# One core of Trainium2: the second product of the attention's scores on 128 rows instead of 64

## The chip, the cores and the metric

The kernel runs on one core of one Trainium2 chip. The metric is the device time of one execution in microseconds (us), as the median of several runs. TensorE (PE) multiplies, its weight loads (PEld) are recorded apart, VectorE (DVE) and ScalarE (ACT) work on elements, GpSimd (POOL) is a third engine for elements, and the queue of SyncE (SP) issues the DMAs.

## The reference

One decoder layer with 1024 tokens and 1024 channels. What the change touches is the differential attention with 4 heads: each head has two maps of scores (queries and keys of 64 channels each, two sets of them), and the two softmaxes are subtracted.

```python
def diff_attention(q1, q2, k1, k2, v, rel_bias, lam):
    ...
        s1 = jnp.einsum('bhqd,bhkd->bhqk', qb1, k1f) * scale + bias
        s2 = jnp.einsum('bhqd,bhkd->bhqk', qb2, k2f) * scale + bias
        p1 = jax.nn.softmax(jnp.where(mask, s1, -1e30), axis=-1)
        p2 = jax.nn.softmax(jnp.where(mask, s2, -1e30), axis=-1)
        return jnp.einsum('bhqk,bhkd->bqhd', p1 - lam * p2, vf)
```

Around it stand a projection `rmsnorm(x) @ w_in`, a pooling and a short convolution beside the attention, the output product `w_o`, a SwiGLU block and a last norm. All data are float32.

## The kernel before

Products are made in three passes: every operand is split into a high half and a low half of few enough bits (float32r), and high x high, high x low and low x high are summed in PSUM. `split_exact` and its relatives do this: ScalarE copies the high half, VectorE subtracts it from the source.

The scores save one pass by stacking halves on the partitions. A query tile `q_tiles[hd, c]` (512 queries) holds for the map s the high half on 64 of the 128 partitions (`ROWS[s]`) and the low half on the other 64. A key tile `k_tiles[hd, c]` holds the high half on both. So one matmul of 128 rows (L496) sums high x high and low x high. The keys' low halves of both maps stand in one tile per head, `k_low[hd]`, map s on the partitions `ROWS[s]`, and a second matmul of 64 rows (L497) adds high x low into the same PSUM bank.

`scores(hd, i)` works on a block of 128 queries and the keys up to it: for each map and each 512 keys, the pair L496, L497; then VectorE adds the bias and takes the maximum (L501, L504, L507), ScalarE takes the exponential (L509), VectorE weighs the two maps (L512, L514, L515). `flip` transposes the result on TensorE (L527) and splits it on ScalarE (L529) and VectorE (L530). `attend` multiplies by v (L540), normalises with an inverse root from GpSimd (`rstd`, L110), and `put` scales on VectorE (L550) and transposes (L552).

The order is written by hand. One iteration of the loop over `early` puts an older block, scores block n, flips and attends block n - 1, and between these it issues steps of a list of projections (`fill_to`, `pace`), which are matmuls of 128 rows (L248, L261, and L199 for v). For each head this list has a column of keys (`done_k`), then a column of queries (`done_q`). The last head's remaining blocks run beside the output product (L616). Then come gate and up (L907) and down (L1016).

Large tiles live in 35 slots of 4 KB per partition (`Slots`), handed out in the order in which they were given back: `sl.new` takes the oldest free slot, `sl.done` returns one. A tile in a reused slot waits for the last readers of the tile before it.

Of the kernel before, what the change touches and what calls it, by code (L numbers as in the profile page):

```python
# [35 lines left out]
# One operand pair per matmul pass: (stationary half, moving half).  # L36
# [11 lines left out]
def split_exact(nc, hi, lo, src, lo_eng):  # L48
    """src = hi + lo exactly, each with few enough bits for a one-pass product."""
    nc.scalar.copy(hi, src)  # L50
    lo_eng.tensor_sub(lo, src, hi.bitcast(F32))  # L51


class Slots:
    """4 KB-per-partition pieces of SBUF, handed out in the order in which they were given back."""
# [16 lines left out]
def tile_hybrid_block(ctx, tc, x, g_mix, w_in, lq1, lk1, lq2, lk2, subln_g, rel_bias, w_pool,  # L72
# [17 lines left out]
    # The tensor engine's clock rises while the first tokens are on their way.  # L90
# [33 lines left out]
    def h_tiles(place):  # L124
        """(hi, lo) for each half of the tokens: [channel in block, block, token]."""
        return [tuple(grp.tile([P, KT, 512], F32R, tag=f"g{2 * place[c] + a}", name=f"h{c}{a}") for a in range(2))
                for c in range(2)]
# [11 lines left out]
    def turn_split(hn, h, t, ks, ps):  # L139
        """h[:, ks, t] = transpose(hn), split; the two instructions that end it."""  # L140
        hi, lo = h[t // 4]
        cols = slice((t % 4) * P, (t % 4 + 1) * P)
        for n, k in enumerate(range(KT)[ks]):
            nc.tensor.transpose(ps[:, n, :], hn[:, k * P:(k + 1) * P], ident)
        return (nc.scalar.copy(hi[:, ks, cols], ps),
                nc.vector.tensor_sub(lo[:, ks, cols], ps, hi[:, ks, cols].bitcast(F32)))

    def transposed(hn, h, t, whole=True):
        """h[:, :, t] = transpose(hn), split; hn is given back."""
        if whole:  # L150
            r = turn_split(hn, h, t, slice(0, KT), bank("a", (P, KT, P)))
        else:
            for n in range(2):
                r = turn_split(hn, h, t, slice(4 * n, 4 * n + 4), bank("c", (P, 4, P)))
        sl.done(hn)
        return r
# [6 lines left out]
    def halves_of(raw, shape, pin=False):  # L163
        """A loaded block of weights as two exact halves."""
        hi = sl.new("w_hi", shape, F32R)
        lo = sl.new("w_lo", shape, F32R)
        ins = nc.scalar.copy(hi, raw)
        if pin:
            tc.keep_in_program_order(ins)
        nc.vector.tensor_sub(lo, raw, hi.bitcast(F32))  # L170
        sl.done(raw)
        return hi, lo
# [69 lines left out]
    def project(w, done):  # L242
        """128 columns of h @ w_in, transposed; done(c, ps) takes each half of the tokens."""
        for c in range(2):
            ps = bank("f")
            for k in range(KT):
                for j, (a, b) in enumerate(PASSES):
                    nc.tensor.matmul(ps, w[a][:, k, :], h[c][b][:, k, :], start=k == 0 and j == 0,  # L248
                                     stop=k == KT - 1 and j == 2)
                yield  # L250
            done(c, ps)
        sl.done(*w)

    def project_pair(ws, dones, between):
        """Two blocks of columns, both for the first half of the tokens before the other half."""
        for c in range(2):
            for w, done in zip(ws, dones):
                ps = bank("f")
                for k in range(KT):
                    for j, (a, b) in enumerate(PASSES):  # L260
                        nc.tensor.matmul(ps, w[a][:, k, :], h[c][b][:, k, :], start=k == 0 and j == 0,  # L261
                                         stop=k == KT - 1 and j == 2)
                    yield
                done(c, ps)
            if c == 0:
                between()
        for w in ws:
            sl.done(*w)
# [7 lines left out]
    def qk_columns(hd):  # L276
        # Both maps' halves side by side on the partitions: [hi; lo] of the first, [lo; hi] of the second.
# [7 lines left out]
        # The high halves of each map twice on the partitions, the low halves of both once.  # L285
        def done_k(c, ps):
            if c == 0:
                k_low[hd] = sl.new("k_low", (P, 2, 512), F32R)
            low = k_low[hd]
            t = k_tiles[hd, c] = sl.new("k", (P, 2, 512), F32R)  # L290
            for s, (own, other) in enumerate((ROWS, ROWS[::-1])):
                nc.scalar.copy(t[own, s, :], ps[own])
                nc.vector.tensor_sub(low[own, c, :], ps[own], t[own, s, :].bitcast(F32))
                nc.vector.tensor_copy(t[other, s, :], t[own, s, :])

# [95 lines left out]
    def chain(items):  # L391
        """Steps of projections, the next one's weights ahead of each one's products.

        What a projection leaves to do (the pool's windows) is spread over the ones after it."""
# [90 lines left out]
    def scores(hd, i):  # L485
# [4 lines left out]
        for s in range(2):  # L490
            ps = bank("a", (P, S))
            q = q_tiles[hd, i // 4][:, s, (i % 4) * P:(i % 4 + 1) * P]
            for c in range((n + 511) // 512):
                w = min(512, n - c * 512)
                part = ps[:, c * 512:c * 512 + w]
                nc.tensor.matmul(part, q, k_tiles[hd, c][:, s, :w], start=True, stop=False)  # L496
                nc.tensor.matmul(part, q[ROWS[s]], k_low[hd][ROWS[s], c, :w], start=False, stop=True)  # L497
# [82 lines left out]
    def split_mixed(c, ms):  # L580
        """Both halves of some of the mixed channels, for one half of the tokens."""
# [44 lines left out]
    # Gate and up are products of 2 by 2 blocks (weights' columns and the channels; the channels and the tokens) in  # L626
    # Winograd's form of Strassen's seven block products. B11, B21: channels of both halves, tokens 512 to 1023;
    # B12, B22: tokens 0 to 511.
# [4 lines left out]
    def split_to(tiles, ps, cols):  # L633
        """Two blocks of 128 channels into each of the tiles."""
        for n, (hi, lo) in enumerate(zip(*tiles)):
            split_exact(nc, hi[:, :, cols], lo[:, :, cols], ps[:, 2 * n:2 * n + 2], nc.vector)

    def turn_early(t):
        """Columns of B11 and B21."""
# [18 lines left out]
    def attend_block():  # L658
        if flipped:
# [3 lines left out]
            for c in over.get((hd, i), ()):  # L663
                sl.done(q_tiles[hd, c], k_tiles[hd, c], v_tiles[hd, c])
                if c == 0:
                    sl.done(k_low[hd])
# [71 lines left out]
    def fetch(m):  # L738
        """Two neighbouring blocks of 128 columns, as two halves of the channels."""
# [44 lines left out]
    def add_rows(t):  # L784
        """The sums of blocks for 128 tokens: T1 = B12 - B11, T2 = T3 + B11, T3 = B22 - B12, T4 = B21 - T2."""
# [74 lines left out]
    # The operands of the last product, two pairs of blocks together: [pair, operand, row, column].  # L860
    kept = {}

    def store(j, names, src):
        """Operands on their way to DRAM: [row, operand, column]."""
# [4 lines left out]
    def store_hidden(j, top, low):  # L869
        """Blocks of the hidden values (tokens; channels) and the sums of them."""  # L870
# [12 lines left out]
    def down_sums(j):  # L883
        """The sums of the blocks (channels; columns) of w_down."""
# [12 lines left out]
    def unit(m, name):  # L897
        """One of the seven products, and what it lets the other engines do."""
# [95 lines left out]
    # Block 1 of the tokens is 512 to 1023; the pairs of blocks of channels are summed two pairs at a time.  # L994
# [24 lines left out]
    def add(i, two, half, ps):  # L1019
        """x2 += ps for a block of tokens and half of the channels."""  # L1020
# [4 lines left out]
    def close(t, r, scaled=False):  # L1025
        """out = x2 * r * g_final; the first half of x2 may have been multiplied by g_final before."""
# [11 lines left out]
    # What of x2 each product is added to, by (second block of tokens, second half of the channels).  # L1038
# [17 lines left out]
    for name in NAMES:  # L1056
# [9 lines left out]
        if final:  # L1066
            # The last block of tokens in two pieces, so that what follows the last product is short.
# [65 lines left out]
def _constants():  # L1133
    """Tables that depend on shapes alone: distances' buckets, the causal mask, window lengths."""
# [33 lines left out]
```

## Time and profile before

| | |
|---|---|
| median of 3 runs | 1117.84 us (1117.19 to 1118.68) |
| span of the profiled execution | 1115.0 us; no other time is given for it |
| TensorE busy | 98% of the span |
| weight loads | 80% |
| VectorE busy | 67% |
| ScalarE busy | 39% |
| GpSimd busy | 4% |

The span runs from the first to the last instruction. A busy share is the union of the times of an engine's instructions; matmuls overlap each other, so the distance between the starts of two of them says more than their lengths. Times in rows are counted from the span's start.

### The profile page before, as it was taken

The page shows a single profiled execution, that of the slowest core. Times are in us where ns is not written, and L with a number is a line of the kernel's source. Part 1 is how long each engine was busy: PE and PEld are TensorE (multiplying, and loading weights), DVE is VectorE, ACT ScalarE, POOL GpSimd, SP SyncE. Part 2 cuts the span into 40 slices and gives each one's busy share as a digit, 9 for nine tenths or more (in the row PEclk, how much of TensorE's full clock was granted, in tenths as well). Part 3 has the DMA queues.
Part 4 walks back from the last instruction along what each step waited for, and adds up shares of the span by engine and source line. Part 5 has one row for each costly group of instructions (what it writes and reads, how often), then busy time and mean ns, then how long its engine had stood idle before and what let it go on. Part 6 is the DMA issues. An engine that isn't in the chain of part 4 may idle for free.

```text
span 1115.0 us, 13835 instructions
## 1 busy us (share of the span) xinstructions
PE 1097.5 (98%) x5215; PEld 896.9 (80%) x5215; DVE 745.7 (67%) x1321; ACT 429.3 (39%) x764; POOL 47.8 (4%) x73
## 2 busy tenths in 40 slices
PE   7999999999999999989999999999999999999997
PEld 7887777797777777868888888888888888888886
DVE  6549567657677565698786768677776668565554
ACT  6325435444544333552332333132323335344342
POOL 1000000000000001120000000000000000000011
PEclk9999999999999999999999999999999999999999
DMA  7301111001125232213554354435544897466553
GB/s 254 102 24 56 39 38 58 19 1 49 39 80 194 76 133 76 91 51 113 198 188 162 111 190 172 162 119 171 179 148 135 294 347 252 155 219 196 190 182 139
DMA packets 96131, 150.60 MB, mean 135 GB/s; under 512 B 7321, under 2 KB 48833, under 8 KB 96065
## 3 DMA queue, kind: packets, MB, share of 16 engines
q1 hardware_dynamic: 96064, 149.72, 40.1%
q8 instruction: 41, 0.67, 0.2%
q14 instruction: 26, 0.20, 0.1%
HBM read 107.49 MB, written 43.00 MB: 135 GB/s over the span
## 4 chain that ended last, share of the span: by engine, by line
PE 94%; DVE 3%; issue 1%; ACT 1%; DMA 0%; POOL 0%; POOLq 0%; DVEq 0%; ACTq 0%
PE ps_f L907 16%; PE ps_f L248 14%; PE ps_a L907 11%; PE ps_c L907 9%; PE ps_a L1016 9%; PE ps_f L616 6%; PE ps_c L1016 5%; PE ps_f L1016 5%; PE ps_f L199 4%; PE ps_a L497 3%; PE ps_c L540 3%; PE ps_a L496 3%; PE ps_f L261 2%; PE ps_c L527 1%; PE ps_a L616 1%
## 5 line engine op out<-in xcount | busy, mean ns | idle before, releaser
L51 DVE TENSOR_TENSOR lo<-raw,hi 128x1024 fp32r<-128x1024 f32 (+1 forms) x84 | 93.0, 1132 | 78.3 <-ACT hi L50 75.9
L248 PE MATMUL ps_f<-h,w_hi 128*128 128x512 f32 x448 | 143.0, 400 | 0.4 <-ACT pt L385 0.4
L50 ACT CAST hi<-raw 128x1024 fp32r<-128x1024 f32 (+1 forms) x84 | 81.5, 980 | 118.2 <-DMA raw<-in_w_down 30.3
L907 PE MATMUL ps_c<-b,w 128*128 128x512 f32 x528 | 124.4, 390 | 0.0
L907 PEld LDWEIGHTS ps_c<-b,w 128*128 128x128 f32 x528 | 98.8, 188 | 20.3
L248 PEld LDWEIGHTS ps_f<-h,w_hi 128*128 128x128 f32 x448 | 80.7, 188 | 19.4 <-issue 2.7
L248 PE MATMUL ps_f<-h,w_lo 128*128 128x512 f32 x224 | 87.5, 391 | 0.0
L110 POOL TENSOR_TENSOR rstd<-ms,nhalf 128x1 f32<-128x1 f32 x56 | 34.6, 618 | 1049.4 <-DVE ms L103 958.5
L51 DVE TENSOR_TENSOR w<-raw,w 128x512 fp32r<-128x512 f32 x66 | 46.5, 705 | 47.5 <-ACT w L50 47.3
L616 PE MATMUL ps_f<-wo_hi,mix 128*128 128x512 f32 x224 | 76.2, 404 | 0.2 <-DVE raw L623 0.2
L50 ACT CAST w_hi<-s 128x1024 fp32r<-128x1024 f32 x44 | 46.0, 1053 | 62.4 <-DVE s L772 55.1
L50 ACT CAST w<-raw 128x512 fp32r<-128x512 f32 x66 | 41.0, 622 | 60.0 <-PE ps_f L907 27.3
L907 PE MATMUL ps_f<-T,w 128*128 128x512 f32 x264 | 63.7, 390 | 0.0
L509 ACT ACTIVATE e<-ps_a,nm 128x128 f32<-128x128 f32 (+7 forms) x64 | 47.2, 744 | 36.8 <-DVE nm L507 36.8
L51 DVE TENSOR_TENSOR w_lo<-s,w_hi 128x1024 fp32r<-128x1024 f32 x44 | 53.4, 1218 | 11.1 <-DMA kept8S<-sum 2.6
L907 PEld LDWEIGHTS ps_f<-T,w 128*128 128x128 f32 x264 | 49.4, 188 | 10.8 <-DVE low L920 0.6
L1016 PE MATMUL ps_a<-lo,hi 128*128 128x512 f32 (+1 forms) x154 | 57.6, 374 | 0.0
L1016 PE MATMUL ps_a<-hi,lo 128*128 128x512 f32 (+1 forms) x154 | 57.6, 374 | 0.0
L1016 PE MATMUL ps_a<-hi 128*128 128x512 f32 (+1 forms) x154 | 57.5, 374 | 0.0
L907 PE MATMUL ps_f<-t,w_hi 128*128 128x512 f32 x176 | 54.5, 389 | 0.0
L907 PE MATMUL ps_a<-t,w_hi 128*128 128x512 f32 x176 | 54.2, 389 | 0.0
L907 PE MATMUL ps_f<-b,w_hi 128*128 128x512 f32 x176 | 54.2, 389 | 0.0
(203 smaller groups left out, 2325.9 us busy)
## 6 DMA issues: line engine op xcount, KB each, us to landing
raw<-in_w_down SPq DMA_DIRECT2D x37, 512.0 KB, 4.5
raw<-in_w_gate SPq DMA_DIRECT2D x22, 512.0 KB, 6.0
raw<-in_w_up SPq DMA_DIRECT2D x22, 512.0 KB, 3.8
raw<-in_w_in SPq DMA_DIRECT2D x20, 512.0 KB, 3.7
raw<-in_x SPq DMA_DIRECT2D x16, 512.0 KB, 4.1
raw<-in_w_o SPq DMA_DIRECT2D x8, 512.0 KB, 5.2
x<-raw SPq DMA_DIRECT2D x8, 512.0 KB, 2.6
x<-x SPq DMA_DIRECT2D x8, 512.0 KB, 5.9
```

Source lines behind the costliest of these rows:

```text
L50: nc.scalar.copy(hi, src)
L51: lo_eng.tensor_sub(lo, src, hi.bitcast(F32))
L110: nc.gpsimd.tensor_tensor(r, ms, nhalf, op=ALU.pow)
L199: nc.tensor.matmul(ps[:, tt, :], h[t // 4][b][:, k, cols], ws[k // 4][a][:, k % 4, :], start=k == 0 and j == 0, stop=k == KT - 1 and j == 2)
L248: nc.tensor.matmul(ps, w[a][:, k, :], h[c][b][:, k, :], start=k == 0 and j == 0, stop=k == KT - 1 and j == 2)
L496: nc.tensor.matmul(part, q, k_tiles[hd, c][:, s, :w], start=True, stop=False)
L497: nc.tensor.matmul(part, q[ROWS[s]], k_low[hd][ROWS[s], c, :w], start=False, stop=True)
L509: nc.scalar.activation(es[:, :n], ps[:, :n], AF.Exp, bias=nm, scale=1.0, accum_out=z[:, s:s + 1])
L540: nc.tensor.matmul(av[:, :(2 - a) * DV], pts[j // 4][:, a, (j % 4) * P:(j % 4 + 1) * P], rhs, start=j == 0 and a == 0, stop=j == i and a == 1)
L616: nc.tensor.matmul(wo_ps[t][nh], halves[m, t // 4][:, a, cols], wo[m][b][:, nh * 512:(nh + 1) * 512], start=m == SET_A[0] and j == 0, stop ...
L907: nc.tensor.matmul(ps, w[a][:, k, :], h[b][k], start=new and k == 0 and j == 0, stop=k == 3 and j == 2, skip_group_check=not new)
L1016: nc.tensor.matmul(ps, a_op[a][:, j, i * P:(i + 1) * P], b_op[b][:, j, cols], start=start and p == 0, stop=stop and p == 2, skip_group_che ...
```

## The change

The low halves of the keys get a tile for each half of the tokens, `k_low[hd, c]`, with the two maps side by side in the free dimension and each map on both halves of the partitions. VectorE writes one half of the partitions as before, GpSimd copies it to the other. The second product then takes the whole query tile as its stationary operand and 128 rows of low halves; it adds low x low to the sum. One more slot is taken per head, and the low halves are given back with the queries, keys and values of their half of the tokens. The rest of the diff removes comments.

```diff
         def done_k(c, ps):
-            if c == 0:
-                k_low[hd] = sl.new("k_low", (P, 2, 512), F32R)
-            low = k_low[hd]
             t = k_tiles[hd, c] = sl.new("k", (P, 2, 512), F32R)
+            low = k_low[hd, c] = sl.new("k_low", (P, 2, 512), F32R)
             for s, (own, other) in enumerate((ROWS, ROWS[::-1])):
                 nc.scalar.copy(t[own, s, :], ps[own])
-                nc.vector.tensor_sub(low[own, c, :], ps[own], t[own, s, :].bitcast(F32))
+                nc.vector.tensor_sub(low[own, s, :], ps[own], t[own, s, :].bitcast(F32))
                 nc.vector.tensor_copy(t[other, s, :], t[own, s, :])
+                nc.gpsimd.tensor_copy(low[other, s, :], low[own, s, :])
...
                 nc.tensor.matmul(part, q, k_tiles[hd, c][:, s, :w], start=True, stop=False)
-                nc.tensor.matmul(part, q[ROWS[s]], k_low[hd][ROWS[s], c, :w], start=False, stop=True)
+                nc.tensor.matmul(part, q, k_low[hd, c][:, s, :w], start=False, stop=True)
...
             for c in over.get((hd, i), ()):
-                sl.done(q_tiles[hd, c], k_tiles[hd, c], v_tiles[hd, c])
-                if c == 0:
-                    sl.done(k_low[hd])
+                sl.done(q_tiles[hd, c], k_tiles[hd, c], k_low[hd, c], v_tiles[hd, c])
```

## Rows read from the trace of the kernel before

**Rows 1.** Page: the span.
```profile
span 1115.0 us, 13835 instructions
```

**Rows 2.** Page: the chain that ended last, by engine.
```profile
PE 94%; DVE 3%; issue 1%; ACT 1%; DMA 0%; POOL 0%; POOLq 0%; DVEq 0%; ACTq 0%
```

**Rows 3.** Stretches: length, PE, PEld, DVE, ACT, POOL busy, granted clock, DMA share, GB/s.
```profile
84.00:112.00 28.00, 28.00 (x125) 21.26 (x125) 25.18 (x68) 15.53 (x40) 1.66 (x3) 1.00 0.20 57
...
76.00:436.00 360.00, 359.49 (x1766) 281.85 (x1766) 242.03 (x621) 159.09 (x386) 22.10 (x37) 1.00 0.19 63
```

**Rows 4.** Timeline of TensorE, block (2,7): start, length, engine, line, operation, shapes.
```profile
306.57 0.50 PE L496 MATMUL ps_a<-k,q 128*128 128x512 f32 x1
307.00 0.49 PE L497 MATMUL ps_a<-k_low,q 64*128 64x512 f32 x1
...
309.12 0.73 PE L248 MATMUL ps_f<-h,w_hi 128*128 128x512 f32 x2
309.69 0.39 PE L248 MATMUL ps_f<-h,w_lo 128*128 128x512 f32 x1
```

**Rows 5.** Timeline of the weight loads there; in brackets the idle time before.
```profile
307.00 0.18 PEld L497 LDWEIGHTS ps_a<-k_low,q 64*128 64x128 f32 x1 [0.24 <-issue]
...
309.46 0.19 PEld L248 LDWEIGHTS ps_f<-h,w_lo 128*128 128x128 f32 x1
```

**Rows 6.** Timeline of TensorE in gate and up, 15 matmuls apart.
```profile
599.92 0.39 PE L907 MATMUL ps_a<-t,w_lo 128*128 128x512 f32 x1
...
603.32 0.39 PE L907 MATMUL ps_f<-b,w_lo 128*128 128x512 f32 x1
```

**Rows 7.** Timeline of TensorE: scores of 384, 256 and 128 columns.
```profile
131.30 0.44 PE L496 MATMUL ps_a<-k,q 128*128 128x384 f32 x1
131.67 0.44 PE L497 MATMUL ps_a<-k_low,q 64*128 64x384 f32 x1
...
245.29 0.38 PE L497 MATMUL ps_a<-k_low,q 64*128 64x256 f32 x1
...
245.92 0.38 PE L497 MATMUL ps_a<-k_low,q 64*128 64x256 f32 x1
...
108.75 0.32 PE L497 MATMUL ps_a<-k_low,q 64*128 64x128 f32 x1
109.00 0.50 PE L496 MATMUL ps_a<-k,q 128*128 128x512 f32 x1
```

**Rows 8.** Timeline of TensorE: products of 128 rows with 256 and 128 columns.
```profile
249.55 0.28 PE L199 MATMUL ps_f<-w_lo,h 128*128 128x256 f32 x1
...
250.63 0.28 PE L199 MATMUL ps_f<-w_lo,h 128*128 128x256 f32 x1
...
309.92 0.93 PE L527 MATMUL ps_c<-ident,e 128*128 128x128 f32 x7
```

**Rows 9.** Timeline of VectorE and GpSimd, before gate and up.
```profile
476.97 0.69 DVE L791 TENSOR_TENSOR t<-hn 128x512 f32<-128x512 f32 x1
...
478.87 1.63 POOL L792 TENSOR_TENSOR t<-hn,t 128x512 f32<-128x512 f32 x1
479.26 1.78 DVE L789 TENSOR_TENSOR t<-hn 128x512 f32<-128x512 f32 x1
```

**Rows 10.** Timeline, block (0,2): first score, weighing, transpose.
```profile
90.94 0.39 PE L496 MATMUL ps_a<-k,q 128*128 128x384 f32 x1
...
97.80 0.62 DVE L515 SCALAR_TENSOR_TENSOR e<-e,t 128x384 f32<-128x384 f32 x1
...
101.82 0.49 PE L527 MATMUL ps_c<-ident,e 128*128 128x128 f32 x3
```

**Rows 11.** Timeline where head 1 ends and head 2 begins.
```profile
240.29 1.08 ACT L529 CAST pT<-ps_c 128x512 fp32r<-128x512 f32 x2
...
242.26 0.34 DVE L515 SCALAR_TENSOR_TENSOR e<-e,t 128x128 f32<-128x128 f32 x1
...
243.14 1.63 PE L540 MATMUL ps_c<-v,pT 128*128 128x256 f32 x13
```

## The prediction

> **What bounds the kernel now.** I read the page first. The chain of work that ended last lies on TensorE for 94% [rows 2] of a span of 1115.0 us [rows 1], so time taken off TensorE's queue counts, as long as no other engine becomes the later one. The second reading is the table by stretches: the scores run from about 76 to 436 us, and there TensorE is busy for 359.49 of 360 us while VectorE is busy for 242.03 [rows 3]. A busy TensorE is not a TensorE at its peak, however, so the third reading is the timeline, for the distance from one matmul's start to the next.
>
> In a block of full length the first products (128 rows) and second products (64 rows) alternate, all 512 columns wide, and start 0.425 us apart (six distances from 306.57 to 309.12 us [rows 4]). The record of the weight loads shows why: the load of each second product begins together with its matmul, at 307.00, after 0.24 us in which the loader waited for nothing the profile shows. Where only 128-row products follow each other, the load for 309.69 begins at 309.46, under the matmul ahead of it [rows 5]. In gate and up, 15 matmuls of 128 rows and 512 columns start between 599.92 and 603.32 us, 0.227 us apart, weight loads and all [rows 6]. The granted clock is 1.00 (2.4 GHz) over the whole stretch of the scores [rows 3], so the clock doesn't explain the difference. What distinguishes the slow pairs is that 128 and 64 rows alternate, and the first matmul after a second product pays too: L248 at 309.12 and its successor take 0.57 us where two take 0.45.
>
> **The change, part by part.** *The second product gets 128 rows.* The number of matmuls and their columns stay; every L497 now has the shape of L496, and no matmul of the attention changes the number of rows. By the loops of scores() L497 runs 96 times: for 4 heads and 2 maps, six products of 512 columns and two each of 384, 256 and 128 over the eight blocks, which makes 48, 16, 16 and 16; L496 does the same. Per width, the distance now and the distance between 128-row matmuls:
> 512 columns: 0.425 against 0.227 us, 0.198 saved, x96 = 19.0 us.
> 384: 0.37 [rows 7]; no 128-row reference, so I take the middle of 0.12 and 0.227, 0.173; 0.197 x32 = 6.3 us.
> 256: 0.315 [rows 7] against 0.12 (L199, nine matmuls from 249.55 to 250.63 [rows 8]); 0.19 x32 = 6.1 us.
> 128: 0.25 [rows 7] against 0.11 (seven transposes of L527 take 0.93 us, three take 0.49 [rows 8, 10]: four more add 0.44); 0.14 x32 = 4.5 us.
> Together 35.9 us. At the ends of a block's scores the distances differ a little: leaving them costs the following matmul 0.11 us today, and the first product of a block meets no switch. For 32 blocks that is +3.5 and about as much in the other direction, so I keep 36 us, with 33 and 39 as bounds.
> Two pages of the Trainium skill differ here. "TensorEngine Tiling (Array Packing)", section Key Properties, says that changing the tiling mode drains the engine; by it the saving is that of the rows. "TensorE: Matmul & The Clock Gate", section "Why this matters for your kernels", says that a single matmul with K=32 takes as long as one with K=128; by that rule alone 64 rows would cost nothing extra and the change would give 0 us. The trace, with 0.425 against 0.227 us, agrees with the first for alternating rows.
>
> *Sixteen copies on GpSimd* (two per call of done_k; 64x512, one input). The trace has none of this kind. From below they cost nothing, since a key column is finished a whole query column ahead of its first scores. From above: GpSimd's L792, 128x512 with two inputs, takes 1.63 us, and a VectorE instruction with two SBUF inputs under it stretches from 0.69 to 1.78 us [rows 9]. Sixteen copies that each hold VectorE up for 1.6 us make 26 us of VectorE time; 242 + 26 = 268 of some 324 us is still not a bound on average. "SBUF — State Buffer", section "Who interferes with whom", calls this an exclusive lock that the later one waits for in full, which agrees with 1.78.
> It can hurt only where VectorE is late already. That is 84 to 112 us (25.18 of 28 us busy [rows 3]), where head 1's keys are split, with four copies. The weighted block of head 0's third block of queries ends on VectorE at 98.42 and TensorE's transpose of it starts at 101.82 [rows 10]: 3.4 us of cover. Four held-up instructions are up to 6.4 us, and the faster TensorE eats about 1 us of the cover per block. GpSimd also gives rstd (L110), and VectorE's L550 queues behind it, with flips and the key splits behind that. I take 1.5 us of loss, bounds 0 and 4 here and 26 for all heads.
>
> *One tile more per head.* Counting new() and done() through the program's order, the free slots of 35 are fewest where block (2,0) follows block (1,7): three are free when the last pT of (1,7) is taken. With heads 1 and 2 both live there are two fewer, so that pT gets the slot of an e of (2,0), which is free only when L515 at 242.26 has ended (242.60). The first attend of (1,7) is at 243.14 [rows 11], and its second pT is read some 0.5 us later, so a copy and a subtract after 242.60 (half of the 1.08 us that L529's pair takes, and about the 0.69 us of [rows 9]) fit nearly. Cost 0 to 1.5 us; I take 0.5. Releasing the low halves with the other tiles of their half merely reorders slots.
>
> *The rest:* the DMAs are the same, the PSUM banks too. Gate, up and down lie behind the attention and move forward as a whole. I take 0.5 us for small waits that come to light in 324 us.
>
> **Sum.** 36 - 1.5 - 0.5 - 0.5 = 33.5 us. The span is 1115.0 us and the median of the runs is 1117.84, so 2.8 us lie around the span; the page gives no other time for the profiled execution, and I keep the 2.8. 1115.0 - 33.5 + 2.8 = 1084.3 us.
>
> **Rivals.**
> A (0.75): as worked out, with 36 +- 3 on TensorE and 0 to 6 us given back: 33 - 6 = 27 to 39, so 1079 to 1091 us. For it: no other engine is above 242 of 360 us.
> B (0.16): VectorE's lateness eats part of it. Each copy holds VectorE for up to 1.6 us, and of these 26 us more than the 6 of A reach TensorE: 36 - 6 to 36 - 26 saved, so more than about 1088 (I draw the line at 1091) and up to 1108 us. For it: 84 to 112 us is nearly full, and in-order VectorE passes a wait on. Against it: outside that stretch VectorE has a third of its time free.
> C (0.04): the change doesn't do what it says: the distance belongs to two products into one bank by one stationary operand, not to the rows. Then 1118 us, or up to 2 more with the copies. Against it: L248 writes 24 products into one bank without it, and the matmul after the pair, in another bank, is hit as well.
> D (0.05): the slots run out, on the other side. With two fewer, the e's of blocks (1,4) to (2,0) could land on slots whose reader belongs to the block before, so that each block's scores wait for the softmax ahead of them. From the first score of block (0,2) at 90.94 to the end of its L515 at 98.42 [rows 10] that is 7.5 us; five blocks lose 37.5 us: 1084.3 + 37.5 = 1121.8 us. It decides only from nearly all five in full, since 33.5 us stand on the other side; the four longer blocks would take more than 7.5 us each. Against it: by the count one slot is still free, and it is one pT that lands on a younger tile, not the e's.
>
> **How the numbers follow.** About 0.2% (2 us) is what a measurement of this kernel can tell from no change. A and B are faster by more: 0.91. C is within: 0.04. D is slower: 0.05. The likeliest case gives 1084.3; its own range is 1079 to 1091. The range for 8 in 10 takes A and half of B: 1079.5 to 1100.
>
> **What would show it.** Right: L497 reads 128x512, its distance to the next matmul falls to 0.227 us, its weight loads start under the matmul before, the "issue" idle time at L496 and L497 is gone, and the last scores come some 33 us earlier. The copies show on GpSimd, with some VectorE instructions near them stretched. Wrong: distances that stay at 0.425 (C); new idle time of TensorE before L527, L540 or L552 released by VectorE (B); or before L496 or L540 at the change from head 1 to head 2 (D).

## The result, and the profile after

The changed kernel takes 1085.03 us (median of 4 runs, 1083.01 to 1085.60) against 1118.26 us before: a ratio of 0.9707, 95% interval 0.9691 to 0.9723, or 33.2 us less. A second measurement (experiment 8) gave 0.9696 (0.9678 to 0.9714). The span of the profiled execution fell from 1115.0 [rows 1] to 1083.3 us.

First the timeline of TensorE over a block of full length, to be laid beside [rows 4] (start, length; the second product is now L496, the first L495):

```profile
283.40 0.39 PE L495 MATMUL ps_a<-k,q 128*128 128x512 f32 x1
283.63 0.39 PE L496 MATMUL ps_a<-k_low,q 128*128 128x512 f32 x1
283.85 0.39 PE L495 MATMUL ps_a<-k,q 128*128 128x512 f32 x1
...
284.76 0.62 PE L248 MATMUL ps_f<-h,w_hi 128*128 128x512 f32 x2
285.21 0.39 PE L248 MATMUL ps_f<-h,w_lo 128*128 128x512 f32 x1
```

Six products of the scores and two of the projection take 285.21 - 283.40 = 1.81 us. In [rows 4] the same eight take 309.69 - 306.57 = 3.12 us. The weight loads there:

```profile
283.18 0.19 PEld L495 LDWEIGHTS ps_a<-k,q 128*128 128x128 f32 x1
283.40 0.19 PEld L496 LDWEIGHTS ps_a<-k_low,q 128*128 128x128 f32 x1
```

The load for the product that starts at 283.63 begins at 283.40, under the product ahead of it. In [rows 5] the load of a second product began with its own product, after 0.24 us of "issue"; that idle time is gone.

The products of 384 columns, for which there was no reference ahead, start 0.17 and 0.18 us apart. The rows are from a block of 896 keys, whose first 512 columns follow in the second map:

```profile
272.82 0.34 PE L495 MATMUL ps_a<-k,q 128*128 128x384 f32 x1
272.99 0.34 PE L496 MATMUL ps_a<-k_low,q 128*128 128x384 f32 x1
273.17 0.40 PE L495 MATMUL ps_a<-k,q 128*128 128x512 f32 x1
```

Not all that TensorE saved came out. The list of waits of the weight loads from 76 to 410 us (who waited for whom: us in total, times, longest) has new entries:

```profile
PEld ps_c L526 <- ACT ps_c L118: 1.8, 2, 1.0
PEld ps_c L526 <- ACT att L562: 1.8, 2, 1.2
PEld ps_f L615 <- ACT mix L50: 1.1, 1, 1.1
PEld ps_f L248 <- DVE w_lo L170: 0.9, 1, 0.9
```

L526 are the transposes of a scored block. They wait for a PSUM bank that `attend` and `put` of older blocks still use on ScalarE: L118 squares the result of `attend` into its bank, L562 reads the bank of `put`. The table by stretches, up to the last attend of each kernel, shows the same from the other side (columns as in [rows 3]; first the kernel before, then the one after):

```profile
76.00:443.40 367.40, 366.67 (x1798) 287.50 (x1798) 246.88 (x631) 161.68 (x393) 23.91 (x39) 1.00 0.20 64
```

```profile
76.00:410.10 334.10, 329.96 (x1799) 281.99 (x1798) 243.71 (x630) 161.12 (x393) 30.70 (x49) 1.00 0.22 70
```

VectorE has nearly the same work in less time, and TensorE is no longer busy all the time: it is idle for 334.10 - 329.96 = 4.1 us where it was idle for 0.7, so 3.4 us of what its products saved did not come out.

What came out can be read off the last attend, again before and after (minimum, median and longest length in ns, first and last start):

```profile
L540 PE MATMUL ps_c<-v,pT x288: 221/280/385, 90.8 to 443.4; 128*128 128x256 f32 x80, 128*128 128x128 f32 x64
```

```profile
L539 PE MATMUL ps_c<-v,pT x288: 221/278/384, 90.2 to 410.1; 128*128 128x256 f32 x80, 128*128 128x128 f32 x64
```

The attention ends 443.4 - 410.1 = 33.3 us earlier. What lies behind it took 1115.0 - 443.4 = 671.6 us and takes 1083.3 - 410.1 = 673.2 us, 1.6 us more. Of the 33.3 us some 1.7 are not the change: in the profiled execution of the kernel before, TensorE's clock fell once during the attention, in that of the changed kernel it did not (last section). Experiment 1, whose products are those of the kernel before and whose profile has no such fall either, starts its last attend at 441.8, 31.7 us behind the changed kernel.

The copies are there as well, on GpSimd (mean 786 ns), and the mean of VectorE's casts beside them has grown from 422 to 468 ns; the third line is that cast in the kernel before:

```profile
L293 POOL CAST k_low<-k_low 64x512 fp32r<-64x512 f32 x16 | 12.6, 786 | 73.5 <-DVE k_low L291 73.5
...
L292 DVE CAST k<-k 64x512 fp32r<-64x512 f32 x16 | 7.5, 468 | 0.5
```

```profile
L294 DVE CAST k<-k 64x512 fp32r<-64x512 f32 x16 | 6.8, 422 | 0.5
```

The mean hides that only two of the sixteen casts grew, to 0.85 and 0.73 us. In these two the copy had started first (85.30 against 85.34 us, and 86.98 against 87.14) and took 0.61 us. Where the cast started first, by 0.03 or 0.10 us, it kept its 0.42 us and the copy beside it took 0.79 to 0.87.

### The profile page after: what moved, and what is told of

Read it like the earlier page. It is cut to its first block, busy times and chain, and to the rows that moved or that the text cites. A ratio compares the mean times of both kernels' runs of the same rounds, so it can differ in the third digit from the quotient of the medians.

```text
span 1083.3 us, 13855 instructions
## 1 busy us (share of the span) xinstructions
PE 1061.3 (98%) x5215; PEld 891.2 (82%) x5215; DVE 745.1 (69%) x1321; ACT 428.1 (40%) x764; POOL 61.4 (6%) x89
## 4 chain that ended last, share of the span: by engine, by line
PE 84%; DVE 9%; DMA 3%; ACT 2%; issue 1%; POOL 0%; POOLq 0%; SPq 0%; DVEq 0%; ACTq 0%
PE ps_f L904 17%; PE ps_a L904 11%; PE ps_f L248 10%; PE ps_c L904 10%; PE ps_a L1013 9%; PE ps_f L615 6%; PE ps_c L1013 5%; PE ps_f L1013 5%; PE ps_f L199 4%; PE ps_c L539 2%; PE ps_c L526 1%; PE ps_a L496 1%; PE ps_a L495 1%; PE ps_f L261 1%; DVE k_low L291 1%
## 5 line engine op out<-in xcount | busy, mean ns | idle before, releaser
L248 PE MATMUL ps_f<-h,w_hi 128*128 128x512 f32 x448 | 140.8, 395 | 0.6 <-ACT pt L384 0.6
```

## The experiments

The times of each group were taken beside runs of the kernel before on the same chip, and the ratio is to those.

**1. The layout without the products.** The changed kernel, with only the second product put back to 64 rows:

```diff
-                nc.tensor.matmul(part, q, k_low[hd, c][:, s, :w], start=False, stop=True)
+                nc.tensor.matmul(part, q[ROWS[s]], k_low[hd, c][ROWS[s], s, :w], start=False, stop=True)
```

> All of the change except its products: the low halves stand twice, with the copies on GpSimd and the extra tile per head, but the second product reads only its 64 rows. Theory (the gain is the 192 changes between 128 and 64 rows, about 0.2 us each, and the copies and tiles cost a little): 1118.3 us plus 0 to 3, so 1118 to 1121, with the distance of full-width products still near 0.425 us. Rival (the gain comes from the new layout, the slots or the order of releases): near 1085 us.

Measured: 1118.06 us, ratio 1.0002 (0.9990 to 1.0014). The copies, tiles and releases cost 0.2 us, give or take 1.3, and win nothing, in a kernel whose second products still have 64 rows. In the timeline the distance is back:

```profile
306.42 0.50 PE L495 MATMUL ps_a<-k,q 128*128 128x512 f32 x1
306.85 0.49 PE L496 MATMUL ps_a<-k_low,q 64*128 64x512 f32 x1
307.27 0.50 PE L495 MATMUL ps_a<-k,q 128*128 128x512 f32 x1
```

The whole gain is in the number of rows of the second product.

**2. The products without the layout.** The kernel before, with a second product of 128 rows that multiplies the high halves of the keys again; it leaves their low halves out of the scores:

```diff
-                nc.tensor.matmul(part, q[ROWS[s]], k_low[hd][ROWS[s], c, :w], start=False, stop=True)
+                nc.tensor.matmul(part, q, k_tiles[hd, c][:, s, :w], start=False, stop=True)
```

> The products alone: the kernel before, whose second product has 128 rows and multiplies the high halves of the keys a second time, so that the low halves are left out of the scores; no copies and no extra tiles. Theory (36 us gross, 2 to 4 us of them given back by copies, tiles and late VectorE): 1082 us, 2 to 4 under the changed kernel. Rival (the copies and tiles are free and the missing part of the gross gain is lost to other waits): the same as the changed kernel, 1085 us within 1.

Measured: 1086.59 us, ratio 0.9725 (0.9710 to 0.9739). Without copies and extra tiles it is not faster than the changed kernel. The theory that they take 2 to 4 us falls, and the rival's number, 1085 us within 1, is missed by 0.6; the missing part of the gross gain goes to other waits. They are not the same ones: here the largest was 2.7 us of the weight loads before L616, for a copy on ScalarE, which the changed kernel has with 1.1 us, and the clock fell behind it (last section). Up to the last attend TensorE is idle for 4.35 us, about as long as in the changed kernel (4.1).

**3. Half as many changes of rows in long blocks.** The kernel before, 64 rows, with the loop over pieces of 512 keys split in two:

```diff
-            for c in range((n + 511) // 512):
-                w = min(512, n - c * 512)
-                part = ps[:, c * 512:c * 512 + w]
+            parts = [(c, ps[:, c * 512:min(n, c * 512 + 512)], min(512, n - c * 512)) for c in range((n + 511) // 512)]
+            for c, part, w in parts:
                 nc.tensor.matmul(part, q, k_tiles[hd, c][:, s, :w], start=True, stop=False)
+            for c, part, w in parts:
                 nc.tensor.matmul(part, q[ROWS[s]], k_low[hd][ROWS[s], c, :w], start=False, stop=True)
```

> The kernel before with 64 rows, but in blocks of more than 512 keys both first products of a map come ahead of both second ones. That leaves out 64 of the 192 changes of rows (4 heads, 4 blocks, 2 maps, 2 changes). Theory (each change costs about 0.2 us): 64 x 0.2 = 12.8 us less, 1105.5 us, and two neighbouring second products of 64 rows start about 0.227 us apart. Rival (64 rows as such are slow): still about 1118 us, and neighbouring 64-row products 0.42 us apart. Rival (two products in a row into one bank): all 36 us or more of these blocks' share gone, with first and second products 0.227 us apart everywhere in them.

Measured: 1106.03 us, ratio 0.9913 (0.9879 to 0.9947). By the ratio that is 9.7 us less (5.9 to 13.5), by the medians 11.4; one of the four runs took 1112.13 us, the others 1105.03 to 1106.74. 12.8 lies inside the interval, 0 and 36 do not. The timeline of one block shows what a change consists of:

```profile
309.30 0.73 PE L497 MATMUL ps_a<-k_low,q 64*128 64x512 f32 x2
309.96 0.73 PE L495 MATMUL ps_a<-k,q 128*128 128x512 f32 x2
310.63 0.73 PE L497 MATMUL ps_a<-k_low,q 64*128 64x512 f32 x2
311.29 0.73 PE L261 MATMUL ps_f<-h,w_hi 128*128 128x512 f32 x2
311.86 0.39 PE L261 MATMUL ps_f<-h,w_lo 128*128 128x512 f32 x1
```

Every pair takes 0.66 to 0.67 us until the next pair, whether it has 64 or 128 rows; two products without a change take 0.454. So a change costs 0.21 us and 64 rows as such cost nothing. The last line splits it: the pair of L261 is left without a change and takes 0.57, so 0.11 us stand at the entry, where the first load begins together with its own product, and the other 0.09 to 0.10 at the end of the pair before. My expectation of 0.227 us between two neighbouring 64-row products missed: they start 0.34 us apart (310.63 and 310.97), and so do the two of 128 rows ahead of them (309.96 and 310.30), since the first of each pair carries its own exposed load. That the engine empties at a change is the likely reason for the other part; the rows show only its length.

**4. The copies on ScalarE.**

```diff
-                nc.gpsimd.tensor_copy(low[other, s, :], low[own, s, :])
+                nc.scalar.copy(low[other, s, :], low[own, s, :])
```

> The changed kernel with the sixteen copies on ScalarE in place of GpSimd. Theory (copies on GpSimd hold VectorE up by a lock and delay rstd, which costs 1 to 3 us): 1082 to 1084 us, and VectorE's cast beside them back at 0.42 us. Rival (the loss is elsewhere): 1085 us or up to 2 more, since ScalarE gets 16 copies of about 0.58 us more in the stretch where it is also needed.

Measured: 1086.54 us, ratio 0.9726 (0.9711 to 0.9740). No gain, although all sixteen casts of VectorE are back at 0.42 us: that VectorE and GpSimd hinder each other in the copies costs no time that shows here. ScalarE has the copies instead (0.62 us each), so a gain below what that costs could be hidden; the theory's 1 to 3 us in the total did not come.

**5. Second products of both maps side by side.** The kernel before, 64 rows; all first products of a block, then the second ones in turn on partitions 0 to 63 and 64 to 127:

```diff
...
                 nc.tensor.matmul(part, q, k_tiles[hd, c][:, s, :w], start=True, stop=False)
-                nc.tensor.matmul(part, q[ROWS[s]], k_low[hd][ROWS[s], c, :w], start=False, stop=True)
+                order.append((c, s, q, part, w))
+        for c, s, q, part, w in sorted(order, key=lambda o: o[:2]):
+            nc.tensor.matmul(part, q[ROWS[s]], k_low[hd][ROWS[s], c, :w], start=False, stop=True)
...
```

> The kernel before with 64 rows; per block all first products of both maps come ahead, then the second products, alternating between map 0 (partitions 0 to 63) and map 1 (64 to 127). Two changes of rows per block in place of four or eight: 64 changes in all against 192. Theory (a change costs 0.1 us for the array to empty and 0.11 us for a weight load that cannot run ahead, and 64 rows as such cost nothing): 128 x 0.2 = 25.6 us under the kernel before, 1092 us, second products 0.227 us apart. Rival 1 (products on different halves of the rows run side by side): pairs of second products start nearly together, 48 x 0.2 to 0.227 us or some 8 us more saved, 1084 us, level with the changed kernel. Rival 2 (64-row products pay the weight load each): second products 0.335 us apart, some 5 us less saved than the theory, 1097 us. In each case up to 2 us come on top because VectorE gets the first map later.

Measured: 1088.82 us, ratio 0.9738 (0.9719 to 0.9757). The timeline decides for the first rival in the products themselves:

```profile
285.03 0.73 PE L499 MATMUL ps_a<-k_low,q 64*128 64x512 f32 x4
285.69 0.73 PE L248 MATMUL ps_f<-h,w_hi 128*128 128x512 f32 x2
286.26 0.40 PE L248 MATMUL ps_f<-h,w_lo 128*128 128x512 f32 x1
```

Four second products take 0.66 us, as long as two did in experiment 3, and they start two by two, at 285.03 and at 285.37: products on different halves of the rows run at the same time. The Trainium skill says so too ("TensorE: Matmul & The Clock Gate", Part 3), and the 0.66 us agree. The rival's 1084 us did not come, however: the kernel is some 4 us behind the changed one. In blocks of up to 512 keys it saves one product of 0.11 to 0.227 us and pays two changes, 0.4 us: 16 blocks lose about 0.2 us each, 3 us, worked out from the rows and not tried apart. The trace agrees in size: the distances from all 192 score products and from the matmul behind each block to their next ones sum to 47.0 us, in the changed kernel to 44.8 without its waits. A wait of 2.33 us and a stretch at half clock behind it (last section) stand in this execution too.

**6. Transposes later.** The changed kernel with `PACE = (0.3, 1.0)` in place of `(0.15, 1.0)`:

> The changed kernel, with 30% in place of 15% of each block's projections issued ahead of the transposes of the block before. Theory (the 4 us that TensorE now waits in the attention are late results of VectorE and ScalarE, which flips and attends meet 1 us earlier per block than before): the transposes get about 1 us more cover and the attends 1 us less, 1 to 2 us saved, 1083 to 1084 us. Rival (the waits are for banks and tiles of other stages, or move from flip to attend): within 1 us of the changed kernel, either way.

Measured: 1081.63 us, ratio 0.9675 (0.9657 to 0.9693); the changed kernel beside it had 0.9696. That is 2.9 us better, and the fastest version of all: its five runs (1081.26 to 1082.70) lie below all eight of the changed kernel (1083.01 to 1085.60). The waits of L526 for a bank have nearly gone (from 76 to 410 us, as above):

```profile
PEld ps_f L248 <- DVE w_lo L170: 0.9, 1, 0.9
...
PEld ps_c L526 <- ACT ps_c L118: 0.2, 1, 0.2
```

and the last attend starts at 407.2:

```profile
L539 PE MATMUL ps_c<-v,pT x288: 222/278/386, 89.8 to 407.2; 128*128 128x256 f32 x80, 128*128 128x128 f32 x64
```

**7. Two slots fewer.** The kernel before with `N_SLOTS = 33`:

> The kernel before with 33 slots in place of 35: what two more tiles take from the pool, through the whole program. Theory (reuse of younger slots costs 0 to 1.5 us in the attention): 1118 to 1120 us. Rival (the slots are a price of their own, as in the case in which each block waits for the softmax ahead of it): more than 1122 us.

Measured: 1121.02 us, ratio 1.0032 (1.0017 to 1.0046), 3 to 4 us. That is more than the theory's 1118 to 1120 and less than the rival's 1122: neither number came. And the time doesn't lie in the attention: the last attend starts at 440.7, not later than the 443.4 of the kernel before, and span less last attend is 680.8 against 671.6 us. In the down product TensorE now waits twice, for 4.7 us together, for a copy on ScalarE before L1016; the kernel before has no such wait.

```profile
core 0 of [0], span 1121.5 us
...
L540 PE MATMUL ps_c<-v,pT x288: 222/278/387, 90.4 to 440.7; 128*128 128x256 f32 x80, 128*128 128x128 f32 x64
```

The changed kernel holds its extra tiles only up to the end of the attention; that it therefore doesn't pay this agrees with experiment 1.

**8. The changed kernel again.**

> The changed kernel on this chip, beside the others: 0.9707 of the kernel before, within 0.002. With copies and tiles at no price, as the layout alone and the products alone have shown, it is level with the products alone, at 0.9725.

Measured: 1084.53 us, ratio 0.9696 (0.9678 to 0.9714), within 0.002 of 0.9707 as expected. The products alone had 0.9725 (0.9710 to 0.9739) on another chip: whether the two are level, the intervals, which just overlap, can't tell.

**9. The other pace in the kernel before.** `PACE = (0.3, 1.0)` alone:

> The kernel before with the pace of 30% alone. Theory (in the kernel before TensorE is slow enough in the scores to hide the late results, so the same cover is worth nothing there): within 1 us of the kernel before. Rival (30% is the better pace for any form of the products, and the 3 us have nothing to do with the change): 3 us less, 1115 us.

Measured: 1118.99 us, ratio 1.0011 (0.9999 to 1.0024). The pace wins nothing there, where TensorE had only 0.7 us of idle time to lose. The 2.9 us of experiment 6 are time that the change made available and that late results had kept back.

**10. Side by side, with that pace.** Experiment 5 with `PACE = (0.3, 1.0)`:

> The side-by-side products of 64 rows (both maps at a time, no copies, one tile per head) with the pace of 30%. Theory (the scores of a block take 1.7 to 1.8 us on TensorE in either form, and the 4 us between them and the changed kernel are results that come late because the first map is finished later): 3 us less than with 15%, 1086 us. Rival (their stretch is simply longer): 1088 to 1089 us as before.

Measured: 1088.95 us, ratio 0.9749 (0.9734 to 0.9764). No gain: the theory falls, and the rival's number came. That the products are behind for their own length alone is not shown: in this execution too TensorE waits 2.54 us before L620 for a copy on ScalarE, with a stretch at half clock behind it, and the pace doesn't move that wait.

**11. Later still.** The changed kernel with `PACE = (0.45, 1.0)`:

> The changed kernel at a pace of 45%. Theory (cover for the transposes is taken from the attends, which have 1 to 4 us of it): by now the attends and the puts are short of it as often, so 1081 to 1084 us, no better than 30%. Rival (more cover for the transposes is better still): 1079 us or less.

Measured: 1083.86 us, ratio 0.9697 (0.9683 to 0.9711). No better than 15%, as the theory had it: what the transposes gain is lost again. From 76 to 412 us the waits of L526 for ScalarE are gone from the list, and longer ones stand at the attends (L539 for VectorE, 1.0 us against 0.2) and at L383 (for ScalarE, 1.5 us against 0.3).

## Why the prediction was right, step by step

*The bound.* TensorE's queue set the time, and it was the distance of starts that mattered. That holds.

*36 us gross.* The block above saved 1.31 us over six changes, leaving included, where the prediction's terms give 6 x 0.198 + 0.11 = 1.30. The guess of 0.173 us for 384 columns was 0.17 to 0.18. Summed over all 192 products and the matmul behind each block, the distances to the next start fall from 80.2 us in experiment 1 to 44.8 in the changed kernel without its waits: 35 us. So 36 was nearly right.

*The cause.* Experiments 1 and 2 pin the gain to the rows of the second product, 3 shows that it goes with the number of changes, and that 64 rows alone are not slow. Rival C is out twice: the result, where two products into one bank by one stationary operand start 0.227 us apart, and experiment 3, where neighbours are in different banks and each change still costs its 0.21 us. What the prediction's 0 us stood for, that a product's time doesn't depend on its rows, is seen in experiment 3 for a product among its like (0.66 us for a pair of either kind); the change beside it costs 0.2 us.

*2.5 us given back.* It was 3.4, and the parts were others. Of the 1.5 us for GpSimd's copies nothing is seen: the layout alone costs 0.2 us within 1.3, the copies on ScalarE are no better, and the products without copies are no faster. A copy takes 0.61 to 0.87 us, half of the 1.63 that bounded it, and the sixteen held VectorE up by 1.6 us in all, not each by up to 1.6: two casts by 0.43 and 0.30 us, and three of the weights' subtractions (L170) by 0.30 each. Of the 0.5 us for slots nothing is seen in the attention. The third part, "small waits that come to light", was set at 0.5 us without a row to it and was nearly all of the 3.4. Experiment 6 shows what most of it is: the transposes reach their PSUM bank before ScalarE and VectorE have left it. The prediction looked at the cover of the weighted block (3.4 us, [rows 10]) but not at that of the bank.

*The sum.* 35 - 3.4 is 31.6 us, which is what the attention gained against experiment 1 (31.7). The prediction had 33.5. That its 1084.3 us came within 0.8 us of the median is in part luck: the fall of the clock in the profiled execution of the kernel before adds 1.7 us to the gain read there, and the 2.8 us "around the span" were too much, since the four runs of the changed kernel took 1.9 to 2.1 us more than their spans. How much of the 33.2 us between the medians is clock is not shown.

*"Gate, up and down move forward as a whole."* They took 1.6 us more in the profiled execution. That can't be laid to the change: span less last attend is 672.6 us in experiment 1, 672.7 in experiment 8 and 673.9 in experiment 9. Which waits make the differences was not tried.

*Rivals B and D.* Late results did eat part of it, but 3.4 and not 6 to 26 us, and the longest waits listed are for ScalarE, not VectorE. The slots did not run out.

## What to carry to other kernels

Look at the distance between starts, and at whether a weight load begins under the matmul ahead of it, before believing that TensorE is full at 98%. Where products with 64 and 128 rows alternate, fill the rows up or group the products; here the padding cost nothing that could be measured (experiment 1), as the columns stayed the same. And when the bound engine becomes faster, set the paces of a hand-written order anew: here that was worth another 2.9 us, and nothing before the change.

## What the runs showed of the hardware that was not expected

Two products of 64 rows on different halves of the partitions, into different banks, run at the same time: four of them in 0.66 us (experiment 5).

TensorE's granted clock fell to its lower level, 1.2 GHz, once during the attention in six of the thirteen profiled executions. In four of them, experiments 2, 3, 5 and 10, it fell right behind a wait of TensorE of 2.21 to 2.54 us, and no other execution has a wait of that length there. For experiment 5 (the stretches' columns as in [rows 3]; the mean clock is the third number from the end):

```profile
328.06 0.49 PE L620 MATMUL ps_f<-wo_hi,mix 128*128 128x512 f32 x1 [2.33 <-ACT mix L50]
...
329.76 1.05 PE L620 MATMUL ps_f<-wo_hi,mix 128*128 128x512 f32 x2
```

```profile
322.00:334.00 12.00, 9.67 (x44) 7.00 (x42) 7.62 (x17) 4.07 (x9) 0.31 (x1) 0.86 0.28 96
```

In the kernel before it fell without an idle stretch, and so it did in experiment 9, both times right behind products that alternate between 128 and 64 rows. In the kernel before these were the eight alternating products of block (3,7):

```profile
321.45 0.50 PE L497 MATMUL ps_a<-k_low,q 64*128 64x512 f32 x1
321.88 1.06 PE L261 MATMUL ps_f<-h,w_hi 128*128 128x512 f32 x2
```

```profile
318.00:326.00 8.00, 8.00 (x30) 5.46 (x29) 4.82 (x13) 3.52 (x9) 0.55 (x1) 0.79 0.00 0
```

From 321.88 on, the two products of L261 take 0.86 us to the next start in place of 0.454. The mean of 0.79 over 8 us means that 0.21 x 8, some 1.7 us, were lost in this execution. The prediction's statement that the clock was at 1.00 over the whole stretch was right only as a rounded mean. Whether the alternating products bring the fall on was not tried; experiments 1 and 7 have the same products and no fall during the attention.
